# MLP norm factor: applied with the ReLU on the sums of the up products instead of on the inputs of the paired blocks

## The chip, the core and the metric

The kernel runs on one core of a Trainium2 chip. A core has five engines that run side by side, each with its own queue that is worked off in order: TensorE (PE, with its weight loads PEld), VectorE (DVE), ScalarE (ACT), GpSimd (POOL) and SyncE (SP), which here issues nearly all DMA transfers. They wait for each other through semaphores. The metric is the device time of one execution in microseconds (us); the kernel before takes 1254.85 us (median of three runs, 1254.52 to 1256.27).

## The reference

Two layers (DEPTH = 2) over 512 tokens of width 1024 in float32. Each layer mixes (attention, short convolution and RWKV heads, then an output projection) and then runs a squared-ReLU MLP behind an RMSNorm. The change touches the MLP alone:

```python
x = x + mixed @ w_out[l]
h = rms_norm(x, norm_mlp_g[l])
x = x + jnp.square(jax.nn.relu(h @ w_mlp_up[l])) @ w_mlp_down[l]
```

`rms_norm(x, g)` is x times a factor per token (one over the root of the mean square) times a weight g per feature. The factor is positive and is the same for all features of a token, so it can stand before or behind the product with `w_mlp_up`, and behind or inside the ReLU.

## The kernel before

Tokens lie on the free axis (512 columns), features on the 128 partitions: x is eight tiles of 128x512. TensorE multiplies in a reduced float32 form, so each operand is split into a high part (`hi`, a cast on ACT) and the rest (`lo`, a subtraction on DVE or POOL), and each product is three matmuls: hi x hi, lo x hi, hi x lo. Weights come in halves of 128x512: SP loads `raw`, ACT casts `whi`, DVE subtracts `wlo`, from rings of three buffers each (`weights`, L328 to L341). A half is used by 12 matmuls. A half's `whi` buffer can be written again only when TensorE has read it.

The mixing part of a layer has an order written out by hand (`ORDER`). It ends with the splits of x times g into `ahif`, `alof` (`inputs`, L721), the first three up products (`up_0` to `up_2`) and the norm's factor (`inner_norm`, L746): sums of squares on TensorE, a power on POOL, then `prbf`, a broadcast of the factor to all partitions in a PSUM bank, and its copy `rsf` in SBUF (L761).

The MLP part has no written order: the program's text is recorded and a scheduler lays the instructions on each engine's queue. It has three sections per layer.

- **The up section.** Eight groups of 128 up features are plain products of `ahif`, `alof` (`up`, L1394). PSUM banks come from a ring of four (`rp`, which `prbf` shares) for all but the first two. DVE multiplies the sum by `rsf` (L1402), ACT applies Relu (L1389), Square (L1391) and the cast `mh` (L1381), POOL makes `ml` (L1382). Meanwhile eight tiles `bn` are made on DVE: x times g times the factor, read from the PSUM bank `prbf` (L1415). From them come four sets of block differences `t` (L1421 to L1424) and their splits `thi`, `tlo` (L1428, L1429).
- **The first down products** (`down`, L1506). Each of eight groups takes 12 matmuls into one of two PSUM banks (`mm`), and DVE adds the sum to x (L1514). Beside them `parts_of` splits `bn` into `bhi`, `blo` (L1437, L1438), in the buffers that `ahif`, `alof` had.
- **The pairs** (`two`, L1440). The remaining 24 up groups are done two at a time with seven products of 256 columns in place of eight (a scheme of Strassen and Winograd): 12 matmuls each, from `bhi`, `blo` or `thi`, `tlo` and from weight sums that DVE makes. DVE adds the pieces to `c0` and `c1` (L1494, L1498, L1501), ACT applies Relu to them and to `pa`. After most pairs come four groups of `down`. There are 12 pairs per layer.

The last layer ends with `last_group` (the last down products, the final norm and the output).

Of the kernel before, what the change touches and what calls it, by code (L numbers as in the profile page):

```python
# [10 lines left out]
F32 = mybir.dt.float32  # L11
F32R = mybir.dt.float32r
# [3 lines left out]
AF = mybir.ActivationFunctionType  # L16
ALU = mybir.AluOpType
# [5 lines left out]
S = 512  # L23
P = 128
NK = D // P
NB = S // P
# [152 lines left out]
N_ONE = 8  # L179
# [7 lines left out]
C_GMIX, C_GMLP, C_SUB, C_CONV, C_MU = 0, 8, 16, 17, 23  # L187
# [81 lines left out]
def tile_trunk(ctx: ExitStack, tc: tile.TileContext, xT, wts, prm_d, cst_d, lora_d, gup_d, lam_d, fin_d, out):  # L269
    nc = tc.nc  # L270
    act, dve, pool = nc.scalar, nc.vector, nc.gpsimd
# [22 lines left out]
    cp = Pool(ctx.enter_context(tc.tile_pool(name="cp", bufs=1)), "cp")  # L294
# [10 lines left out]
    x = [cp.tile([P, S], F32, tag=f"x{j}", name=f"x{j}") for j in range(NK)]  # L305
# [58 lines left out]
    nrm = {}  # L364
# [198 lines left out]
    for l in range(L):  # L563
# [5 lines left out]
        with ExitStack() as mx:  # L569
# [176 lines left out]
            def inner_norm():  # L746
                key = f"f{l}"
                yield from got(nrm, "all" + key)
                pt = psum("rp", 4, f"pss{key}")
                for b in range(NB):  # L750
                    ins = pe.matmul(pt[:, b:b + 1], nrm[key][0][:, b * P:(b + 1) * P], ones1, start=True, stop=True)
                yield ins
                r = cp.tile([P, NB], F32, tag="rr", bufs=2, name=f"rr{key}")
                yield from root_steps(r, pt[:, :NB], NB)
                rb = psum("rp", 4, f"prb{key}")
                for b in range(NB):
                    ins = pe.matmul(rb[:, b * P:(b + 1) * P], r[:, b:b + 1].to_broadcast([P, P]), ident, start=True, stop=True)
                yield ins
                rs = cp.tile([P, S], F32, tag="rs", bufs=1, name=f"rs{key}")
                nrm["rs"] = rs, rb  # L760
                yield act.copy(rs, rb)  # L761

            def norm():
# [604 lines left out]
        with ExitStack() as mx:  # L1368
# [2 lines left out]
            H = S // 2  # L1371
            mids = []

            rs, rb = nrm["rs"]

            def kept(m):

# [7 lines left out]
            def square(cs, name):  # L1385

                r = fp.tile([P, S], F32, tag="r", bufs=2, name=f"r{name}")
                for i, c in enumerate(cs):
                    act.activation(r[:, i * H:i * H + c.shape[1]], c, AF.Relu)  # L1389
                m = fp.tile([P, S], F32, tag="m", bufs=3, name=f"m{name}")  # L1390
                act.activation(m, r, AF.Square)  # L1391
                kept(m)

            def up(i):  # L1394

                if i < NUP:
                    pt = ups[i]
                else:
                    pt = psum("rp", 4, f"up{l}_{i}")
                    mm3(pt, weights(wbase + NG_IN + NG_OUT + i), acts)  # L1400
                c = fp.tile([P, S], F32, tag="c0", bufs=2, name=f"c{l}_{i}")
                dve.tensor_tensor(c, pt, rs, ALU.mult)  # L1402
                square([c], f"{l}_{i}")

            bn, th = {}, {}

            def scaled_by_norm(j):
                if j == 0:  # L1410
                    fp.tile([P, 8], F32, tag="pad0", name=f"pad0_{l}")
                bn[j] = fp.tile([P, 2, H], F32, tag="shi" if j < 5 else "slo", bufs=5, name=f"bn{l}_{j}")
                if j == 5:
                    fp.tile([P, 24], F32, tag="pad1", name=f"pad1_{l}")
                dve.scalar_tensor_tensor(bn[j].rearrange("p a s -> p (a s)"), x[j], pr[:, C_GMLP + j:C_GMLP + j + 1], rb,  # L1415
                                         ALU.mult, ALU.mult)

            def blocks(k):
                b1, b2 = bn[k], bn[k + 4]
# [11 lines left out]
            bs = {}  # L1431

            def parts_of(j):

                n = 1 if j < 4 else 2
                hi, lo = bs[j] = [cp.tile([P, 2, H], F32R, tag=f"a{p}{j}", name=f"b{p}{l}_{j}") for p in ("hi", "lo")]
                act.copy(hi[:, :n], bn[j][:, :n])  # L1437
                dve.tensor_tensor(lo[:, :n], bn[j][:, :n], hi[:, :n].bitcast(F32), ALU.subtract)  # L1438

            def two(i0, i1):  # L1440

                n = f"{l}_{i0}"
                wg = wbase + NG_IN + NG_OUT

                def raw(i, a):
                    t = fp.tile([P, 4, P], F32, tag="sraw", bufs=6, name=f"raw{n}_{i}_{a}")
                    nc.sync.dma_start(t.rearrange("p k c -> p (k c)"), wts[wg + i, :, a * P:(a + 4) * P])
                    return t

                def both(src, name):  # L1450
                    hi, lo = [fp.tile([P, 4, P], F32R, tag=f"s{p}", bufs=5, name=f"s{p}{n}_{name}") for p in ("hi", "lo")]
                    act.copy(hi, src)  # L1452
                    dve.tensor_tensor(lo, src, hi.bitcast(F32), ALU.subtract)  # L1453
                    return hi, lo

                def sum_(name, a, b, op):
                    t = fp.tile([P, 4, P], F32, tag=name, name=f"{name}{n}")
                    dve.tensor_tensor(t, a, b, op)
                    return t

                def small(name):
                    return fp.tile([P, H], F32, tag=name, bufs=2, name=f"{name}{n}")

                def product(pt, w, moving, first=True):

                    whi, wlo = w
                    for k in range(4):
                        ahi, alo = moving(k)
                        pe.matmul(pt, whi[:, k], ahi, start=(first and k == 0), stop=False, skip_group_check=True)
                        pe.matmul(pt, whi[:, k], alo, start=False, stop=False, skip_group_check=True)  # L1470
                        pe.matmul(pt, wlo[:, k], ahi, start=False, stop=(k == 3), skip_group_check=True)

                blk = lambda d, q: lambda k: [p[:, q] for p in bs[4 * d + k]]
                smm = lambda q: lambda k: [p[:, q] for p in th[k]]
                pa, pb = [psum("rp", 4, f"p{i}{n}")[:, :H] for i in "ab"]
                pc = psum("at", 2, f"pc{n}")[:, :H]
                c0 = fp.tile([P, S], F32, tag="c0", bufs=2, name=f"c0{n}")
                w11 = raw(i0, 0)
                product(pa, both(w11, "p1"), blk(0, 0))
                p1 = small("p1")  # L1480
                act.copy(p1, pa)
                w21 = raw(i1, 0)
# [11 lines left out]
                dve.tensor_tensor(c0[:, :H], pc, p1, ALU.add)  # L1494
# [6 lines left out]
                dve.tensor_tensor(c0[:, H:], pb, u2, ALU.add)  # L1501
                square([c0], f"{n}_0")
                product(pa, both(w22, "p4"), smm(3), False)
                square([pa, c1], f"{n}_1")

            def down(h, js):  # L1506

                g, k0 = h // 2, 4 * (h % 2)
                for j in js:
                    pt = psum("mm", 2, f"dn{l}_{h}_{j}")  # L1510
                    mm3(pt, weights(wbase + NG_IN + NG_OUT + NG_UP + 8 * g + j, k0, k0 + 4), mids[4 * h:4 * h + 4], 4)
                    if h == 0:
                        parts_of(j)
                    dve.tensor_tensor(x[j], pt, x[j], ALU.add)  # L1514
# [12 lines left out]
            for p in range(N_TWO):  # L1527
# [76 lines left out]
```

## Time and profile before

| what | value |
|---|---|
| median of three runs | 1254.85 us (1254.52 to 1256.27) |
| the profiled execution | 1255.07 us, of which span 1253.1 us; 2.0 us lie around the span |
| granted TensorE clock | 0.997 of full speed |
| DMA | 127.92 MB, mean 102 GB/s |
| layer 0: up section, first down products, pairs | from about 291, 326.6 and 349.5 us |
| layer 1: the same | from about 907.5, 945.8 and 967.7 us |

A row of the engines' line gives busy time, its share of the span and the number of instructions. Rows of the timeline give start, duration, engine, line, operation, output<-inputs and, in brackets, how long the engine sat idle before it and what ended that. TensorE's matmuls overlap: one of 512 columns is shown as 0.39 us long, while the next starts 0.23 us later, so the distance from start to start is the measure of its pace.

### The profile page before, as it was taken

What the parts mean: (1) busy time and instruction counts of PE and PEld (TensorE: products, weight loads), DVE (VectorE), ACT (ScalarE), POOL (GpSimd) and SP (SyncE); (2) the same over time, 40 slices, a digit from 0 to 9 for tenths busy, and PEclk for the clock granted to TensorE, in tenths of its full rate; (3) what the DMA queues carried; (4) which work ended last, traced back from release to release, by engine and by line L of the source; (5) the groups of instructions that cost most, each with busy time, mean ns of one, the idle gap of its engine ahead of it and who ended that gap; (6) DMA issues with size and microseconds to landing.
All of it is one profiled execution on the core that took longest, in us unless ns stands there. A gap on an engine that the chain in (4) does not pass through costs nothing. (4 is left out here: it accounts for less than half of the span.)

```text
span 1253.1 us, 25011 instructions
## 1 busy us (share of the span) xinstructions
PE 1233.6 (98%) x9493; PEld 1055.0 (84%) x9493; DVE 903.3 (72%) x1731; ACT 697.5 (56%) x1476; POOL 358.2 (29%) x461
## 2 busy tenths in 40 slices
PE   9999999999999999999999999999999999999997
PEld 6888788788799999999778887888878999998987
DVE  6887888768967676764666777887598666666654
ACT  6785655546645454544475656464565545454553
POOL 1264637332301010101225455464221111111100
PEclk9999999999999999999999999999999999999998
DMA  6523323142332323221235233232423232323122
GB/s 214 162 91 93 113 87 107 53 143 84 128 100 94 110 93 110 93 93 35 78 109 161 80 119 108 91 88 71 141 84 135 93 109 94 108 95 108 53 76 76
DMA packets 84696, 127.92 MB, mean 102 GB/s; under 512 B 21472, under 2 KB 25568, under 8 KB 84576
## 3 DMA queue, kind: packets, MB, share of 16 engines
q1 hardware_dynamic: 83856, 125.77, 31.4%
q8 instruction: 75, 1.23, 0.4%
q10 hardware_dynamic: 720, 0.55, 0.1%
q14 instruction: 45, 0.37, 0.1%
HBM read 117.11 MB, written 9.18 MB: 101 GB/s over the span
## 5 line engine op out<-in xcount | busy, mean ns | idle before, releaser
L1382 POOL TENSOR_TENSOR ml<-m,mh 128x512 fp32r<-128x512 f32 x64 | 93.4, 1461 | 500.7 <-ACT mh L1381 482.7
L338 ACT CAST whi<-raw 128x512 fp32r<-128x512 f32 x142 | 88.0, 621 | 174.4 <-PE dn L282 159.0
L282 PE MATMUL dn<-mh,whi 128*128 128x512 f32 x448 | 175.1, 391 | 1.2 <-DVE x L1514 1.2
L282 PE MATMUL dn<-ml,whi 128*128 128x512 f32 x448 | 174.6, 390 | 0.0
L282 PE MATMUL dn<-mh,wlo 128*128 128x512 f32 x448 | 174.6, 390 | 0.0
L674 POOL TENSOR_TENSOR wlo<-raw,whi 128x512 fp32r<-128x512 f32 x84 | 110.5, 1316 | 189.2 <-ACT whi L662 159.4
L282 PE MATMUL pj<-ahim,whi 128*128 128x512 f32 x392 | 156.6, 399 | 1.0 <-DVE x L1514 0.9
L282 PE MATMUL pj<-ahim,wlo 128*128 128x512 f32 x392 | 156.7, 400 | 0.0
L282 PE MATMUL pj<-alom,whi 128*128 128x512 f32 x392 | 156.0, 398 | 0.0
L662 ACT CAST whi<-raw 128x512 fp32r<-128x512 f32 x142 | 87.5, 617 | 85.8 <-PE pj L282 29.8
L1514 DVE TENSOR_TENSOR x<-dn,x 128x512 f32<-128x512 f32 x112 | 76.7, 686 | 77.4 <-PE dn L282 77.4
L339 DVE TENSOR_TENSOR wlo<-raw,whi 128x512 fp32r<-128x512 f32 x142 | 113.4, 799 | 11.3 <-ACT whi L338 10.7
L1453 DVE TENSOR_TENSOR slo_p<-s,shi_p 128x512 fp32r<-128x512 f32 x96 | 70.9, 741 | 63.4 <-ACT shi_p L1452 60.8
L282 PEld LDWEIGHTS dn<-mh,whi 128*128 128x128 f32 x448 | 84.1, 188 | 19.9 <-issue 2.0
L282 PEld LDWEIGHTS dn<-mh,wlo 128*128 128x128 f32 x448 | 84.1, 188 | 17.9
L282 PEld LDWEIGHTS dn<-ml,whi 128*128 128x128 f32 x448 | 84.1, 188 | 16.5
L1452 ACT CAST shi_p<-s 128x512 fp32r<-128x512 f32 x96 | 59.1, 617 | 49.7 <-PE pa L282 38.1
L282 PEld LDWEIGHTS pj<-ahim,whi 128*128 128x128 f32 x392 | 73.8, 188 | 15.1 <-ACT whi L662 1.3
L282 PEld LDWEIGHTS pj<-alom,whi 128*128 128x128 f32 x392 | 73.9, 189 | 14.0 <-issue 0.5
L282 PEld LDWEIGHTS pj<-ahim,wlo 128*128 128x128 f32 x392 | 73.8, 188 | 14.0 <-DVE wlo L674 0.2
L282 PE MATMUL pa<-tlo,shi_p 128*128 128x256 f32 x288 | 81.4, 282 | 0.0
L282 PE MATMUL pa<-thi,shi_p 128*128 128x256 f32 x288 | 81.2, 282 | 0.0
(416 smaller groups left out, 3232.5 us busy)
## 6 DMA issues: line engine op xcount, KB each, us to landing
raw<-wts SPq DMA_DIRECT2D x389, 256.0 KB, 2.7
qs<-dqhi SPq DMA_DIRECT2D x24, 128.0 KB, 3.7
ks<-dkhi SPq DMA_DIRECT2D x24, 128.0 KB, 4.0
x<-xT SPq DMA_DIRECT2D x8, 256.0 KB, 4.6
dqhi<-qhi SPq DMA_DIRECT2D x6, 256.0 KB, 3.3
dqlo<-qlo SPq DMA_DIRECT2D x6, 256.0 KB, 3.4
dkhi<-khi SPq DMA_DIRECT2D x6, 256.0 KB, 2.7
dklo<-klo SPq DMA_DIRECT2D x6, 256.0 KB, 3.5
```

The lines of the kernel that those rows point to most:

```text
L282: ins = nc.tensor.matmul(*a, **k)
L338: act.copy(hi[:, :n], raw[:, :n])
L339: (pool if a and lean[0] else dve).tensor_tensor(lo[:, :n], raw[:, :n], hi[:, :n].bitcast(F32), ALU.subtract)
L662: yield act.copy(hi[:, k0:k1], raw[:, k0:k1])
L674: yield eng.tensor_tensor(lo[:, k0:k1], raw[:, k0:k1], hi[:, k0:k1].bitcast(F32), ALU.subtract)
L1382: pool.tensor_tensor(lo, m, hi.bitcast(F32), ALU.subtract)
L1452: act.copy(hi, src)
L1453: dve.tensor_tensor(lo, src, hi.bitcast(F32), ALU.subtract)
L1514: dve.tensor_tensor(x[j], pt, x[j], ALU.add)
```

## The change

The factor leaves the blocks' inputs and is applied to the sums, in the same instruction as the ReLU: `r = max(sum, 0) * rs`, on DVE, for the plain groups and for the pairs. So the pairs' blocks can be x times g without the factor: the products of plain blocks read `ahif`, `alof` (no second split, `parts_of` is gone), and `bn` is now made on ACT. Its bias operand `none`, a column of zeros computed from `rs`, makes it wait until the factor exists. The column takes one of the two buffers of the ring `rr`, which a table-loading Sqrt (L468, output `rrF`) uses too.

```diff
-                nrm["rs"] = rs, rb
+                nrm["rs"] = rs
...
-            rs, rb = nrm["rs"]
+            rs = nrm["rs"]
...
                 r = fp.tile([P, S], F32, tag="r", bufs=2, name=f"r{name}")
                 for i, c in enumerate(cs):
-                    act.activation(r[:, i * H:i * H + c.shape[1]], c, AF.Relu)
+                    q = slice(i * H, i * H + c.shape[1])
+                    dve.scalar_tensor_tensor(r[:, q], c, 0.0, rs[:, q], ALU.max, ALU.mult)
...
-                c = fp.tile([P, S], F32, tag="c0", bufs=2, name=f"c{l}_{i}")
-                dve.tensor_tensor(c, pt, rs, ALU.mult)
-                square([c], f"{l}_{i}")
+                square([pt], f"{l}_{i}")
...
+            none = cp.tile([P, NB], F32, tag="rr", bufs=2, name=f"none{l}")[:, :1]
+            dve.tensor_scalar(none, rs[:, :1], 0.0, None, ALU.is_lt)
-            def scaled_by_norm(j):
+            def by_gain(j):
...
-                dve.scalar_tensor_tensor(bn[j].rearrange("p a s -> p (a s)"), x[j], pr[:, C_GMLP + j:C_GMLP + j + 1], rb,
-                                         ALU.mult, ALU.mult)
+                act.activation(bn[j].rearrange("p a s -> p (a s)"), x[j], AF.Identity, scale=pr[:, C_GMLP + j:C_GMLP + j + 1],
+                               bias=none)
...
-            def parts_of(j):
-                n = 1 if j < 4 else 2
-                hi, lo = bs[j] = [cp.tile([P, 2, H], F32R, tag=f"a{p}{j}", name=f"b{p}{l}_{j}") for p in ("hi", "lo")]
-                act.copy(hi[:, :n], bn[j][:, :n])
-                dve.tensor_tensor(lo[:, :n], bn[j][:, :n], hi[:, :n].bitcast(F32), ALU.subtract)
...
-                blk = lambda d, q: lambda k: [p[:, q] for p in bs[4 * d + k]]
+                blk = lambda d, q: lambda k: [p[:, q * H:(q + 1) * H] for p in acts[4 * d + k]]
...
-                    if h == 0:
-                        parts_of(j)
...
-                for j in range(2 * max(i - 2, 0), min(2 * max(i - 1, 0), NK)):
-                    scaled_by_norm(j)
                 if i >= N_ONE - 4:
-                    blocks(i - N_ONE + 4)
+                    k = i - N_ONE + 4
+                    by_gain(k)
+                    by_gain(k + 4)
+                    blocks(k)
```

The scheduler lays the queues anew. Three places, as they stand before and after.

TensorE, layer 1, where `up_2` ends (a row's first name is the sum, behind the arrow the tokens' part and the weights' part). Before:

```order
L282 MATMUL up_2_11687<-alof_7_11628,whi_4_11671 128x512
L282 MATMUL up_2_11687<-ahif_7_11627,wlo_4_11673 128x512
L282 MATMUL up_4_11803<-ahif_0_11418,whi_0_11806 128x512
L282 MATMUL up_4_11803<-alof_0_11419,whi_0_11806 128x512
L282 MATMUL up_4_11803<-ahif_0_11418,wlo_0_11807 128x512
```

After:

```order
L282 MATMUL up_2_11641<-alof_7_11582,whi_4_11625 128x512
L282 MATMUL up_2_11641<-ahif_7_11581,wlo_4_11627 128x512
L282 MATMUL up_3_11697<-ahif_0_11372,whi_0_11700 128x512
L282 MATMUL up_3_11697<-alof_0_11373,whi_0_11700 128x512
L282 MATMUL up_3_11697<-ahif_0_11372,wlo_0_11701 128x512
```

Before, the first half of `up_4` stood ahead of all of `up_3`; now it stands behind it. All other matmuls of the kernel keep their order (those of the pairs with `ahif`, `alof` in the place of `bhi`, `blo`).

DVE, layer 0, where the first down group is added to x (`x_69` is the first tile of x). Before:

```order
L339 TENSOR_TENSOR wlo_0_4534<-raw_0_4531,whi_0_4533 128x512
L1438 TENSOR_TENSOR blo_6_4646<-bn_6_4348,bhi_6_4645 128x512
L1438 TENSOR_TENSOR blo_7_4670<-bn_7_4350,bhi_7_4669 128x512
L1514 TENSOR_TENSOR x_69<-dn_0_0_4482,x_69 128x512
L1453 TENSOR_TENSOR slo_8_p_4681<-raw_8_8_0_4678,shi_8_p_4680 128x512
L339 TENSOR_TENSOR wlo_0_4558<-raw_0_4555,whi_0_4557 128x512
L1453 TENSOR_TENSOR slo_8_p_4705<-s_8_4702,shi_8_p_4704 128x512
L1453 TENSOR_TENSOR slo_8_p_4725<-s_8_4722,shi_8_p_4724 128x512
L1514 TENSOR_TENSOR x_70<-dn_0_1_4506,x_70 128x512
```

After:

```order
L1390 SCALAR_TENSOR_TENSOR r_7_4444<-up_7_4407,rsf_4109 128x512
L339 TENSOR_TENSOR wlo_0_4512<-raw_0_4509,whi_0_4511 128x512
L1505 TENSOR_TENSOR x_69<-dn_0_0_4468,x_69 128x512
L339 TENSOR_TENSOR wlo_0_4532<-raw_0_4529,whi_0_4531 128x512
L1505 TENSOR_TENSOR x_70<-dn_0_1_4488,x_70 128x512
```

The eight `blo` are gone, and the splits of the first pair's weights (`slo_8`) have moved up into the up section; between two sums added to x stands one `wlo`.

DVE, layer 0, the end of the third pair (number 10) and the start of the down groups behind it. Before:

```order
L1501 TENSOR_TENSOR c_10_5155<-pb_10_5153,u_10_5218 128x256
L1458 TENSOR_TENSOR s_12_5678<-s_12_5658,raw_12_12_0_5634 128x512
L1453 TENSOR_TENSOR slo_11_p_5462<-raw_11_11_4_5459,shi_11_p_5461 128x512
L1453 TENSOR_TENSOR slo_11_p_5481<-s_11_5478,shi_11_p_5480 128x512
L1514 TENSOR_TENSOR x_69<-dn_2_0_5311,x_69 128x512
L339 TENSOR_TENSOR wlo_0_5375<-raw_0_5372,whi_0_5374 128x512
```

After:

```order
L1494 TENSOR_TENSOR c_10_5109<-pb_10_5107,u_10_5172 128x256
L1451 TENSOR_TENSOR s_12_5632<-s_12_5612,raw_12_12_0_5588 128x512
L1390 SCALAR_TENSOR_TENSOR r_10_0_5232<-c_10_5109,rsf_4109 128x512
L1390 SCALAR_TENSOR_TENSOR r_10_1_5256<-pa_10_5106,rsf_4109 128x256
L1390 SCALAR_TENSOR_TENSOR r_10_1_5256<-c_10_5211,rsf_4109 128x256
L1446 TENSOR_TENSOR slo_11_p_5416<-raw_11_11_4_5413,shi_11_p_5415 128x512
L1446 TENSOR_TENSOR slo_11_p_5435<-s_11_5432,shi_11_p_5434 128x512
L1451 TENSOR_TENSOR s_12_5671<-raw_12_12_0_5588,raw_12_24_0_5608 128x512
L1505 TENSOR_TENSOR x_69<-dn_2_0_5265,x_69 128x512
```

Three instructions `r` stand in the queue ahead of the next pair's splits; the second of them waits for the pair's last product in `pa`.

More of the change, by code (lines that the diff above doesn't have):

```diff
@@ L1400, in up @@
                     mm3(pt, weights(wbase + NG_IN + NG_OUT + i), acts)
-                c = fp.tile([P, S], F32, tag="c0", bufs=2, name=f"c{l}_{i}")
-                dve.tensor_tensor(c, pt, rs, ALU.mult)
-                square([c], f"{l}_{i}")
+                square([pt], f"{l}_{i}")
             bn, th = {}, {}
-            def scaled_by_norm(j):
+            none = cp.tile([P, NB], F32, tag="rr", bufs=2, name=f"none{l}")[:, :1]
+            dve.tensor_scalar(none, rs[:, :1], 0.0, None, ALU.is_lt)
+            def by_gain(j):
                 if j == 0:
                     fp.tile([P, 8], F32, tag="pad0", name=f"pad0_{l}")
-                bn[j] = fp.tile([P, 2, H], F32, tag="shi" if j < 5 else "slo", bufs=5, name=f"bn{l}_{j}")
-                if j == 5:
+                bn[j] = fp.tile([P, 2, H], F32, tag="shi" if j < 4 else "slo", bufs=5, name=f"bn{l}_{j}")
+                if j == 4:
                     fp.tile([P, 24], F32, tag="pad1", name=f"pad1_{l}")
-                dve.scalar_tensor_tensor(bn[j].rearrange("p a s -> p (a s)"), x[j], pr[:, C_GMLP + j:C_GMLP + j + 1], rb,
-                                         ALU.mult, ALU.mult)
+                act.activation(bn[j].rearrange("p a s -> p (a s)"), x[j], AF.Identity, scale=pr[:, C_GMLP + j:C_GMLP + j + 1],
+                               bias=none)
             def blocks(k):
@@ L1429, in blocks @@
                     dve.tensor_tensor(lo[:, u], t[i], hi[:, u].bitcast(F32), ALU.subtract)
-            bs = {}
-            def parts_of(j):
-                n = 1 if j < 4 else 2
-                hi, lo = bs[j] = [cp.tile([P, 2, H], F32R, tag=f"a{p}{j}", name=f"b{p}{l}_{j}") for p in ("hi", "lo")]
-                act.copy(hi[:, :n], bn[j][:, :n])
-                dve.tensor_tensor(lo[:, :n], bn[j][:, :n], hi[:, :n].bitcast(F32), ALU.subtract)
             def two(i0, i1):
```

## Prediction

> **What bounds the kernel now.** I read the page's totals, then its chain of waits, then what TensorE itself waited for, and last the timeline at those places.
>
> ```profile
> span 1253.1 us, 25011 instructions
> PE 1233.6 (98%) x9493; PEld 1055.0 (84%) x9493; DVE 903.3 (72%) x1731; ACT 697.5 (56%) x1476; POOL 358.2 (29%) x461
> ...
> PE 37%; DVE 1%; ACT 0%; issue 0%; POOL 0%; POOLq 0%; DVEq 0%
> ...
> 945.83 21.83 PE dn L282 x96
> ...
> 977.66 10.93 PE dn L282 x48
> ```
>
> The chain lies on TensorE almost alone, and in the pairs and the down groups it has no holes: 48 matmuls take 10.93 us, 0.228 us each. The change leaves their number as it is, so a saving on DVE or ACT is worth only what it closes of TensorE's holes, and a cost there is free until it opens one. The waits of TensorE in the MLP are few:
>
> ```profile
> PE dn L282 <- DVE x L1514: 1.2, 3, 0.7
> PE up L282 <- DVE wlo L339: 0.9, 1, 0.9
> PE up L282 <- ACT whi L338: 0.5, 1, 0.5
> PE up L282 <- DVE bn L1415: 0.4, 1, 0.4
> ```
>
> Their places, from TensorE's timeline, the `up` rows in layer 1, the `dn` rows in layer 0:
>
> ```profile
> 915.61 0.39 PE L282 MATMUL up<-ahif,wlo 128*128 128x512 f32 x1
> 916.53 0.50 PE L282 MATMUL up<-ahif,whi 128*128 128x512 f32 x1 [0.53 <-ACT whi L338]
> 916.86 0.40 PE L282 MATMUL up<-alof,whi 128*128 128x512 f32 x1
> 918.14 0.50 PE L282 MATMUL up<-ahif,wlo 128*128 128x512 f32 x1 [0.88 <-DVE wlo L339]
> ...
> 920.32 0.39 PE L282 MATMUL up<-ahif,wlo 128*128 128x512 f32 x1
> 921.09 0.47 PE L282 MATMUL up<-ahif,whi 128*128 128x512 f32 x1 [0.38 <-DVE bn L1415]
> ...
> 331.77 0.39 PE L282 MATMUL dn<-mh,wlo 128*128 128x512 f32 x1
> 332.82 0.47 PE L282 MATMUL dn<-mh,whi 128*128 128x512 f32 x1 [0.66 <-DVE x L1514]
> ...
> 335.42 0.39 PE L282 MATMUL dn<-mh,wlo 128*128 128x512 f32 x1
> 335.83 0.47 PE L282 MATMUL dn<-mh,whi 128*128 128x512 f32 x1
> ```
>
> Each hole is the distance of two starts less 0.23. Around 916 us: 0.92, 0.33 and 1.28 make 0.69 + 0.10 + 1.05 = 1.84 us. At 921: 0.77, so 0.54. In layer 0: 1.05 and 0.41, so 0.82 + 0.18 = 1.00. Together 3.38 us. Behind them stands a full DVE in the up section, and an idle one in the pairs (its busy time in a stretch of each):
>
> ```profile
> 293.00:326.00 33.00, 32.53 (x56) 1.00 0.30 99
> ...
> 967.66:988.59 20.93, 14.27 (x23) 1.00 0.31 100
> ```
>
> **The change part by part: what closes.** The 1.84 us are a matter of order. `up_4`'s first half follows `up_2` at once, and its `whi` needs the buffer that `up_2`'s last half has just given back:
>
> ```profile
> 915.86 0.62 ACT L338 CAST whi<-raw 128x512 fp32r<-128x512 f32 x1 [1.58 <-issue]
> ```
>
> ACT casts it 0.25 us after TensorE's last start there, DVE's `wlo` comes later still. Now `up_3` stands there; its first half gets the buffer of `up_2`'s first half, 12 matmuls (2.7 us) earlier, and `up_4` starts 24 matmuls later. I count all 1.84 us as gained. The 0.54 us are the PSUM bank of `prbf`, held until the last `bn` has read it. After the change its only reader is the copy `rsf`, so it is free some 12 us before: 0.54 gained. The 1.00 us in layer 0 are DVE's backlog:
>
> ```profile
> 330.80 1.28 DVE L1438 TENSOR_TENSOR blo<-bn,bhi 128x512 fp32r<-128x512 f32 x2
> 332.00 0.68 DVE L1514 TENSOR_TENSOR x<-dn,x 128x512 f32<-128x512 f32 x1
> ```
>
> The first down sum waits behind `blo`, and TensorE's third group for its bank. The `blo` go, and so do the eight `bn` from DVE's queue:
>
> ```profile
> L1415 DVE SCALAR_TENSOR_TENSOR bn<-x,prm,prbf 128x512 f32<-128x512 f32 x16 | 11.2, 738 | 0.0
> ...
> L1438 DVE TENSOR_TENSOR blo<-bn,bhi 128x512 fp32r<-128x512 f32 x8 | 5.1, 679 | 0.0
> ```
>
> Per layer that is 8 x 0.74 = 5.9 and, with four `blo` of 512 columns and four of 256 (taken at half), 2.7 + 1.4 = 4.1 us less; the eight `r` that replace the `c` cost 0 to 0.06 us more each (0.68 of L1438's row to 0.74 of L1415's). About 9.5 us less on DVE, ahead of the sum that was late by some 2 us: 1.00 gained.
>
> **What is added.** Bounds from the nearest rows:
>
> ```profile
> L1389 ACT ACTIVATE r<-c 128x512 f32<-128x512 f32 x40 | 25.3, 633 | 19.0 <-DVE c L1402 9.5 <-DVE c L1501 8.9
> ...
> L730 ACT ACTIVATE ahif<-x,prm 128x512 fp32r<-128x512 f32 x16 | 11.0, 714 | 1.8 <-PE po L282 1.2 <-DVE x L715 0.6
> ...
> L915 ACT ACTIVATE t<-av,drv,prm 128x512 f32<-128x512 f32 x6 | 4.8, 803 | 0.0
> ...
> L1494 DVE TENSOR_TENSOR c<-pc,p 128x256 f32<-128x256 f32 x24 | 10.2, 424 | 5.9 <-PE pc L282 5.9
> ...
> L468 ACT ACT_TABLE_LOAD x1 | 1.3, 1283 | 0.0
> ```
>
> *`bn` on ACT* lies between L730 (one column operand, 0.71) and L915 (two, 0.80); it has two, so 0.80, eight times 6.4 us per layer, against eight Relu less (5.0): +1.4 us, and the eight `bhi` go behind it. The column `none` (four bytes a partition on DVE) is 0.1 to 0.2 us and delays the first `bn` alone. *The Sqrt table* is loaded before at the start of layer 1 and, after other tables, once more at the end, where ACT is waiting anyway; now it is loaded once, behind `rsf` in layer 1: 1.28 us plus 0.2 for `rrF` on ACT, at a delicate place. I place it by hand:
>
> ```profile
> 907.82 0.59 ACT L761 COPY rsf<-prbf 128x512 f32<-128x512 f32 x1 [0.88 <-PE prbf L282]
> ```
>
> `rsf` ends at 908.4, the table and `rrF` at 909.9, then a Square, `bn`, `mh`, Square, `whi` (second half of `up_3`), `mh`, and `whi` of its first half: at 0.63 us each (0.80 for `bn`) 914.5. TensorE gets there at 915.61 + 0.23 = 915.84. So 1.3 us are in hand, 0.4 to 0.5 more for the `wlo` behind it, which TensorE needs two matmuls later and DVE makes at 0.68 us. Between 0 and the whole 1.5 us may come through; I take 0.
>
> *The pairs.* DVE gets one `r` of 512 and two of 256 columns per pair: 0.74 + 0.42 + 0.42 = 1.6 us (1.5 by the `TENSOR_TENSOR` rows), ACT loses its Relus. DVE has 20.93 - 14.27 = 6.7 us idle in such a period, so its total fits. What counts is the queue, since the second `r` waits for the pair's last product and the splits and x sums stand behind it:
>
> ```profile
> 421.64 0.68 DVE L1458 TENSOR_TENSOR s<-s,raw 128x512 f32<-128x512 f32 x1
> ...
> 425.07 0.90 DVE L1453 TENSOR_TENSOR slo_p<-s,shi_p 128x512 fp32r<-128x512 f32 x1 [2.15 <-ACT shi_p L1452]
> 425.89 0.68 DVE L1514 TENSOR_TENSOR x<-dn,x 128x512 f32<-128x512 f32 x1
> ...
> 428.21 0.69 DVE L1514 TENSOR_TENSOR x<-dn,x 128x512 f32<-128x512 f32 x1
> ```
>
> The 1.6 us fall into the 2.15 us in which DVE waits for a cast that ACT makes late, behind Relus and Squares; without the Relus that cast comes before the Squares. Without this cover the x sum would end at 426.6 + 1.6 = 428.2, about when the third down group needs its bank (the second's sum can start at 428.21), so even then little shows. I take 0; were all 1.6 us to come through in 24 pairs, it would be 38 us. POOL's and SP's queues have the same work; a few loads for the second pair are issued earlier.
>
> **Sum.** 1255.07 - 1.84 - 0.54 - 1.00 = 1251.7 us for an execution like the profiled one (span 1249.7). The median of the runs is 0.2 below it, so **1251.5 us**.
>
> **The rivals.**
>
> *The holes only move (20%).* For it: three weight buffers per ring leave TensorE two halves ahead, whatever the order; ACT and DVE now hand `bn`, `t`, `thi`, `tlo` to each other with the `whi` and `wlo` queued between them. Against it: 9.5 us less on DVE. If the 1.84 us stay as another wait, the run gives 1251.5 + 1.8 = 1253.3; if all stay, the change does nothing for the time: 1254.85.
>
> *ACT becomes late in the up section (12%, slower).* Place: `whi` behind `bn`, which waits for the factor. Price: if in each of the four block steps one `bn` and one `t` to `thi` handover (0.8 + 0.7 us) stay ahead of the `whi` that TensorE needs, that is 6 us per layer, less the 1.3 us in hand and the two halves of lead (2.7 us): 2 us per layer beyond the old holes, 4 in all: 1254.85 + 4 = 1259. It decides from 1.3 us on. Against it: behind the place in question ACT (the fourth pair of numbers) is far from full:
>
> ```profile
> 921.00:946.00 25.00, 24.91 (x110) 20.67 (x111) 22.85 (x39) 17.83 (x34) 6.02 (x5) 1.00 0.29 95
> ```
>
>
> *DVE's queue in the pairs opens a hole in each (5%, slower).* Place: the x sum behind `r`, price: what it is late beyond 1.6 us, in 22 periods with down groups. For it, POOL and DVE stretch each other:
>
> ```profile
> L1453 DVE TENSOR_TENSOR slo_p<-s,shi_p x96: 675/693/1348, 333.8 to 1191.4; 128x512 fp32r<-128x512 f32 x96
> ```
>
> If `r` stretched so, 0.65 us more, then 22 x 0.65 - 3.4 = 11 us: 1266. Against it: in the trace POOL's `ml` of a pair comes only after that pair's `r`. The Trainium skill ("SBUF — State Buffer", "Who interferes with whom") says that a VectorE instruction with two SBUF inputs and a GpSimd instruction that reads SBUF exclude each other for the whole instruction; that speaks against the change, since two of the three `r` have two SBUF inputs where ACT's Relu had one. The largest value in the row, 1348 ns beside a median of 693, agrees with it; by that rule the 11 us would follow only if `r` met `ml`.
>
> **How the numbers follow.** The forecast has 63%: 1250 to 1252.6 by itself (an unseen small start more or less). The range reaches over the moved holes up to 1256 and down to 1249.8; most of the two slower cases stays outside. A measurement here tells about 0.2%, 2.5 us, from no change: faster is below 1252.3, nearly all of the forecast and a little of the second case (61%); same is the rest of both (22%); slower 17%.
>
> **What would show it.** TensorE's waits: the four rows above gone, the first pair of layer 1 about 2.4 us earlier after `prbf` than now, that of layer 0 1.0 us. DVE in a pair period near 15.9 us of 20.93, with `r` inside the wait before the x sum. Wrong would be: a wait of `up` for `whi` or `wlo` of another group, a `dn` that waits for x behind a pair, or a pair period longer than 20.93 us.

## The result, and the profile after

The changed kernel takes 1252.11 us (median of 22 runs), the kernel before 1254.01 us in the same comparison; the ratio is 0.9981 with a 95% interval of 0.9974 to 0.9989, so 1.4 to 3.3 us are gained. A second comparison, with the experiments below, has 1250.62 against 1254.37 us, 0.9973 (0.9963 to 0.9983). The forecast was 1251.5 us.

The page of the changed kernel, its totals (engine, busy us, share of the span, instructions):

```profile
span 1252.3 us, 24947 instructions
PE 1234.0 (99%) x9493; PEld 1057.9 (84%) x9493; DVE 915.4 (73%) x1773; ACT 665.7 (53%) x1386; POOL 374.2 (30%) x461
```

TensorE does the same work; DVE has 42 instructions more and ACT 90 fewer. The two profiled spans alone (1253.1 and 1252.3 us) would hide most of the result, because single executions of one kernel lie 5 to 6 us apart in the first comparison. So the profiles are read stretch by stretch, between starts of TensorE's instructions that both kernels have. What TensorE waited for in the changed kernel's MLPs (us in total, times, longest), all rows on `up`, `dn` and `pa`:

```profile
PE up L282 <- DVE wlo L339: 0.6, 1, 0.6
...
PE dn L282 <- DVE x L1505: 0.5, 2, 0.3
PE pa L282 <- DVE c L1491: 0.4, 1, 0.4
```

The waits for `whi` and `bn` are gone, and of the `dn` rows only two small ones are left, at the very end of layer 0, where before has them too (0.17 and 0.32 us). The `wlo` and the `pa` row are new ones. TensorE's timeline at the old places, layer 1 at 916 us and layer 0 at 331 us, shows the closed holes as an even pace:

```profile
916.81 0.39 PE L282 MATMUL up<-ahif,whi 128*128 128x512 f32 x1
917.04 0.39 PE L282 MATMUL up<-alof,whi 128*128 128x512 f32 x1
917.27 0.39 PE L282 MATMUL up<-ahif,wlo 128*128 128x512 f32 x1
...
331.31 0.39 PE L282 MATMUL dn<-mh,wlo 128*128 128x512 f32 x1
331.54 0.39 PE L282 MATMUL dn<-mh,whi 128*128 128x512 f32 x1
```

And the two new holes, at the end of layer 1's up section and in layer 0's first pair:

```profile
941.52 0.39 PE L282 MATMUL up<-alof,whi 128*128 128x512 f32 x1
942.46 0.51 PE L282 MATMUL up<-ahif,wlo 128*128 128x512 f32 x1 [0.55 <-DVE wlo L339]
942.80 0.40 PE L282 MATMUL up<-ahif,whi 128*128 128x512 f32 x1
...
356.32 0.28 PE L282 MATMUL pb<-ahif,slo_p 128*128 128x256 f32 x1
356.97 0.39 PE L282 MATMUL pa<-thi,shi_p 128*128 128x256 f32 x1 [0.37 <-DVE c L1491]
```

Here is the reason of the first one. DVE's timeline, and below it POOL's, in the 2.5 us ahead of it:

```profile
939.43 0.68 DVE L1446 TENSOR_TENSOR slo_p<-raw,shi_p 128x512 fp32r<-128x512 f32 x1
940.03 1.77 DVE L1446 TENSOR_TENSOR slo_p<-s,shi_p 128x512 fp32r<-128x512 f32 x1
941.73 0.68 DVE L339 TENSOR_TENSOR wlo<-raw,whi 128x512 fp32r<-128x512 f32 x1
```

```profile
939.41 1.84 POOL L1382 TENSOR_TENSOR ml<-m,mh 128x512 fp32r<-128x512 f32 x1 [1.66 <-ACT mh L1381]
```

The two `slo_p` have one shape. The first starts with POOL's `ml` and takes 0.68 us, while that `ml` takes 1.84 us where the shortest takes 1.29. The second takes 1.77 us and ends 0.55 us after `ml` does. So DVE and POOL seem to take turns here. The `wlo` that TensorE needs stands behind the second: 1.1 us too late. The second hole is a load that lands late: DVE's sum for the third pair waits for it, and this pair's `c` stands behind that sum.

The stretches, in us, are the basis of all that follows: "up" from the first `prbf` matmul to the first down matmul, "down" from there to the first pair, "pair 1" from there to the second pair; "MLPs" is both layers from `prbf` to their ends (layer 0: the next layer's first mixing product; layer 1: the last sums of the norm). E5 and E4 are second profiles of the kernel before and of the change.

| kernel | layer 0: up | down | pair 1 | layer 1: up | down | MLPs | ratio to before (95%) |
|---|---|---|---|---|---|---|---|
| before | 36.51 | 23.19 | 20.92 | 39.04 | 21.83 | 670.6 | |
| E5, before again | 36.51 | 23.20 | 20.93 | 39.06 | 21.76 | 670.7 | 0.9994 (0.9984 to 1.0003) |
| the change | 36.64 | 21.77 | 21.57 | 37.29 | 21.77 | 668.5 | 0.9981 (0.9974 to 0.9989) |
| E4, the change again | 36.61 | 21.77 | 21.65 | 37.25 | 21.77 | 668.5 | 0.9973 (0.9963 to 0.9983) |
| E1, bank free early | 37.18 | 23.09 | 20.92 | 37.26 | 23.94 | 672.3 | 1.0010 (1.0000 to 1.0021) |
| E2, plain groups only | 36.51 | 22.91 | 20.93 | 39.82 | 22.03 | 672.3 | 1.0022 (1.0011 to 1.0033) |
| E3, pairs and blocks only | 36.59 | 22.46 | 21.63 | 36.46 | 23.62 | 670.2 | 1.0002 (0.9991 to 1.0013) |
| E6, `bn` on DVE | 37.93 | 22.18 | 20.92 | 37.74 | 22.52 | 670.4 | 0.9994 (0.9983 to 1.0004) |
| E7, `none` by itself | 37.51 | 21.78 | 21.65 | 37.38 | 21.77 | 669.2 | 1.0023 (1.0012 to 1.0033) |
| E8, `ml` on DVE | 36.51 | 21.77 | 20.93 | 36.41 | 21.77 | 666.5 | 0.9961 (0.9949 to 0.9973) |
| E9, pairs' `r` twice | 36.61 | 21.76 | 21.62 | 37.26 | 21.76 | 669.4 | 0.9984 (0.9973 to 0.9996) |
| E10, plain `r` twice | 36.51 | 23.41 | 20.93 | 36.79 | 24.15 | 671.0 | 1.0001 (0.9991 to 1.0011) |
| E11, `none` in an old buffer | 36.64 | 21.76 | 21.67 | 36.79 | 21.77 | 667.9 | 0.9970 (0.9960 to 0.9980) |
| E12, before with `ml` on DVE | 36.51 | 21.77 | 20.93 | 39.45 | 21.77 | 670.5 | 0.9993 (0.9983 to 1.0003) |

Two profiles of one kernel agree within 0.1 us in the MLPs, and the MLPs' sum goes roughly with the measured ratio. The exception is E7, which loses elsewhere. One of the eleven executions of E7 took 4279 us and is not in its ratio. The change gains 2.2 us there, 0.6 in layer 0 and 1.6 in layer 1.

### The profile page after: what moved, and what is told of

It is laid out like the page before. It is cut to its first block, busy times and chain, and to the rows that moved or that the text cites. A ratio compares the mean times of both kernels' runs of the same rounds, so it can differ in the third digit from the quotient of the medians.

```text
span 1252.3 us, 24947 instructions
## 1 busy us (share of the span) xinstructions
PE 1234.0 (99%) x9493; PEld 1057.9 (84%) x9493; DVE 915.4 (73%) x1773; ACT 665.7 (53%) x1386; POOL 374.2 (30%) x461
## 5 line engine op out<-in xcount | busy, mean ns | idle before, releaser
L1382 POOL TENSOR_TENSOR ml<-m,mh 128x512 fp32r<-128x512 f32 x64 | 110.3, 1739 | 481.2 <-ACT mh L1381 375.4
L1446 DVE TENSOR_TENSOR slo_p<-s,shi_p 128x512 fp32r<-128x512 f32 x96 | 67.9, 708 | 18.1 <-ACT shi_p L1445 15.5
```

The lines of the kernel that those rows point to most:

```text
L1382: pool.tensor_tensor(lo, m, hi.bitcast(F32), ALU.subtract)
```

## The experiments

### E1 to E4: the parts of the change

One caution holds for all that follows. For every altered program the scheduler lays the queues of DVE, ACT and SP anew, so an experiment changes a load and the order of these queues together. TensorE's order stays one of two: before's in E2 and E12, the change's in all others, E1 included (E5 and E4 repeat their kernels).

Theory at this point: a part of the sum belongs to the bank of `prbf` and can be had alone. In E1, `bn` reads the copy `rsf` in SBUF; nothing else in the program's text differs from before:

```diff
-                nrm["rs"] = rs, rb
+                nrm["rs"] = rs
...
-            rs, rb = nrm["rs"]
+            rs = nrm["rs"]
...
-                dve.scalar_tensor_tensor(bn[j]..., x[j], pr[:, C_GMLP + j:C_GMLP + j + 1], rb,
+                dve.scalar_tensor_tensor(bn[j]..., x[j], pr[:, C_GMLP + j:C_GMLP + j + 1], rs,
```

> Before, with one thing changed: bn reads the SBUF copy rsf instead of the PSUM bank of prbf. Theory (the bank): with the copy as the bank's only reader, up_3's first half stands ahead of up_4's again, and both layer-1 holes go: from prbf to the first matmul of the first pair it is 58.5 us (before 60.87, less 1.84 and 0.54); layer 0 keeps its two dn holes (1.00 us); the time is 2.4 us below before, ratio 0.9981. Rival (the holes come from DVE's and ACT's load, which this leaves as it is): the stretch stays above 60 us, with up waiting for whi or wlo of another group, ratio 0.9995 to 1.0.

Layer 1's up stretch is 37.26 us, as short as the change's: the order is back to `up_3` ahead of `up_4`, and both holes are gone. So who reads the bank is what had turned the order. But nothing is gained. TensorE's timeline in layer 1's first down groups:

```profile
950.65 0.39 PE L282 MATMUL dn<-mh,wlo 128*128 128x512 f32 x1
952.47 0.47 PE L282 MATMUL dn<-mh,whi 128*128 128x512 f32 x1 [1.43 <-DVE x L1514]
```

TensorE arrives 1.8 us earlier and finds DVE as late as ever, with the last five `blo` (2.9 us) still queued ahead of the first x sum: the down stretch grows from 21.8 to 23.94 us. The theory names the cause of the two holes and is wrong on their price.

E2 is before with the plain groups' `r` on DVE, all else as it was; E3 is the reverse, the change with the plain groups as before. This is E2's main cut (`squared` is the part of `square` behind the ReLU):

```diff
-                c = fp.tile([P, S], F32, tag="c0", bufs=2, name=f"c{l}_{i}")
-                dve.tensor_tensor(c, pt, rs, ALU.mult)
-                square([c], f"{l}_{i}")
+                r = fp.tile([P, S], F32, tag="r", bufs=2, name=f"r{l}_{i}")
+                dve.scalar_tensor_tensor(r, pt, 0.0, rs, ALU.max, ALU.mult)
+                squared(r, f"{l}_{i}")
```

> Before, with only the plain up groups changed: DVE's r (ReLU times factor) in place of DVE's c and ACT's Relu; bn, parts and pairs as before. Theory (the bank): bn still reads the bank, up_4's first half still stands ahead of up_3, DVE's queue is as full as before: the stretch prbf to first pair of layer 1 60.3 to 60.9 us, layer 0 keeps its dn holes, ratio 0.9995 to 1.0005. Rival (the holes come from ACT's casts behind its Relus): whi is earlier by up to a Relu (0.63 us), the stretch below 60.2 us, ratio 0.9990 or less.

> The change without its first part: pairs and blocks as in the change (bn without the factor, on ACT; r with the factor on DVE in the pairs; bhi and blo gone), plain up groups as before (c on DVE, Relu on ACT). Theory: nearly all of the change's gain is here: layer 0's dn holes gone (1.0 to 1.3 us), layer 1's 1.84 and 0.54 gone; ratio 0.9975 to 0.9985. If the wlo hole at the end of layer 1's up section (0.83 us in the change's profile) comes from POOL's ml beside DVE's full queue, it stays within 0.4 us of that; if it comes from r with its two inputs in the plain groups, it is gone. Rival (the gain needs the plain groups' r): ratio 0.9990 or more.

E2 loses: its holes at 916 to 921 us are the same ones, two of them larger (`wlo` 1.20 us, `bn` 0.84 us), and the `whi` wait is unchanged at 0.5 us, so ACT's Relus were not what held the casts. E3 gains nothing that the runs can tell. It has the shortest up stretch of layer 1 but for one (36.46 us) and no `wlo` hole there, and then loses 1.9 us in the down groups:

```profile
947.07 0.39 PE L282 MATMUL dn<-ml,whi 128*128 128x512 f32 x1
948.14 0.50 PE L282 MATMUL dn<-mh,wlo 128*128 128x512 f32 x1 [0.68 <-DVE wlo L339]
```

DVE's rows ahead of this hole are of the kind seen in the change. A weight sum `s` takes 1.54 us where others take 0.68, it ends 0.56 us after an `ml` of POOL (945.49 to 946.93), and the awaited `wlo` stands behind it:

```profile
945.95 1.54 DVE L1459 TENSOR_TENSOR s<-raw,raw 128x512 f32<-128x512 f32 x1 [0.17 <-DMA raw<-wts]
947.41 0.68 DVE L339 TENSOR_TENSOR wlo<-raw,whi 128x512 fp32r<-128x512 f32 x1
```

So alone the first half of the change loses 1.6 us in the MLPs and the second gains 0.5; together they gain 2.2. Of the four theories only E3's rival, that the gain needs the plain groups' `r`, fits its ratio; both of E2's missed. Why the plain groups' `r` is a loss with the old blocks and a gain with the new ones was not taken further apart.

> The changed kernel once more, unaltered, for a second profile. Theory: the wlo hole at the end of layer 1's up section is the order's and stays (0.6 to 1.0 us in starts); the stretch at the granted clock of 0.5 to 0.75 after the sums of layer 1's mixing norm, the late load at 686 us and the late loads in the first pairs are this one execution's and are gone or elsewhere: from layer 0's last down group to prbf of layer 1 as before (289.1 us within 0.5) instead of 2.2 us longer. Rival (they belong to the change): all of them at the same places. Ratio 0.9975 to 0.9988.

The changed kernel again, unaltered: the `wlo` hole is there (0.55 us idle), and so is the late load in layer 0's first pair (0.47); they belong to the change. The slow stretch and the late load in layer 1's mixing are gone (280.76 us from layer 0's end to `prbf`, where the first profile took 284.12 and before 281.91): these were that execution's.

### E5, E6, E10, E12: DVE's load

New theory: the holes are DVE's backlog; where they open is the order's doing, how large they are in sum is DVE's whole time from `prbf` to the first pair. E5 is the kernel before once more:

> The kernel before once more, unaltered, as a null test and for a second profile. From prbf to the first mixing product of the next layer 334.7 us in layer 0, from prbf to the last sums of the norm 335.95 us in layer 1, both within 0.4 us; the mixing of layer 1 281 to 284 us, with or without a stretch at half the granted clock after its sums; ratio 0.9990 to 1.0010. Rival (the profile of before was an exception): the holes at 916 to 921 us of layer 1 differ by more than 0.5 us in sum.

It repeats the first profile within 0.1 us in every stretch. E6 takes the change and puts `bn` back on DVE, E10 makes each plain `r` twice, E12 takes the kernel before and makes the plain groups' `ml` on DVE:

```diff
-                act.activation(bn[j]..., x[j], AF.Identity, scale=pr[:, C_GMLP + j:C_GMLP + j + 1], bias=none)
+                dve.tensor_scalar(bn[j]..., x[j], pr[:, C_GMLP + j:C_GMLP + j + 1], none, ALU.mult, ALU.add)
```

> The change with its eight bn per layer put back on DVE (one input times the column), ACT freed of them; bhi and blo stay gone. Theory (DVE's whole load of the up section and first down group sets the holes): 3.3 to 5.9 us more on DVE per layer bring back 1 to 2.5 us of holes over the two layers, in the up section or in the first down sums; ratio 0.9980 to 1.0000. Rival (the order of the weights halves alone): no more holes than the change has, ratio 0.9970 to 0.9980.

```diff
-                    dve.scalar_tensor_tensor(r[:, q], c, 0.0, rs[:, q], ALU.max, ALU.mult)
+                    for _ in range(2 if name in plain else 1):
+                        dve.scalar_tensor_tensor(r[:, q], c, 0.0, rs[:, q], ALU.max, ALU.mult)
```

> The change with each r of the plain up groups made twice on DVE (eight times 0.68 = 5.4 us more per layer, same values). Theory (DVE's whole load of the up section sets the holes): 1 to 2 us more per layer, layers' MLP together 670.5 to 672.5 us where the change has 668.5; ratio 0.9990 to 1.0015. Rival (what the change gained is the order of the weights' halves and the bank alone): MLP together within 0.6 us of the change's, ratio 0.9965 to 0.9985.

```diff
-                pool.tensor_tensor(lo, m, hi.bitcast(F32), ALU.subtract)
+                (dve if i < N_ONE else pool).tensor_tensor(lo, m, hi.bitcast(F32), ALU.subtract)
```

> The kernel before with the ml of the plain up groups on DVE instead of POOL, nothing else. Theory (POOL's ml costs DVE as much as making ml itself): DVE is no later than before, layer 0's first down group 22.0 to 23.2 us (23.2 before); layer 1 keeps its order and bank holes, 38.0 to 39.2 us from prbf to the first down group; ratio 0.9985 to 1.0000. Rival (this alone gives what the change gives): 36.5 to 37.3 us there, ratio 0.9980 or less.

Read together, from one row each (`plain` in E10's cut holds the names of the plain groups): busy times in layer 1 from `prbf` to the first pair (the stretch, its length, then PE, PEld, DVE, ACT, POOL with their instructions, the granted clock, DMA share and GB/s). Before (E5):

```profile
905.22:966.04 60.82, 59.02 (x260) 48.05 (x261) 52.62 (x87) 37.01 (x68) 14.41 (x9) 1.00 0.35 109
```

The change (E4):

```profile
903.94:962.96 59.02, 58.47 (x260) 48.22 (x261) 45.62 (x72) 35.53 (x62) 16.28 (x9) 1.00 0.37 112
```

E3:

```profile
907.66:967.74 60.08, 59.03 (x261) 48.06 (x262) 45.74 (x72) 39.53 (x70) 14.57 (x9) 1.00 0.35 111
```

E6:

```profile
904.49:964.75 60.26, 59.14 (x261) 48.03 (x261) 50.38 (x80) 30.65 (x54) 15.44 (x9) 1.00 0.34 110
```

E10:

```profile
904.87:965.81 60.94, 59.19 (x260) 48.00 (x261) 50.05 (x80) 35.07 (x62) 17.29 (x9) 1.00 0.36 108
```

The third pair of numbers, DVE, goes with the length in four of these rows, though not in proportion: 45.6 us and 59.0; 50.1 to 50.4 and 60.3 to 60.9; 52.6 and 60.8. Eight more instructions of 0.68 us on DVE (E10) cost 1.9 us here and 2.5 us in both MLPs, the whole gain. Eight `bn` of 0.6 us more on DVE (E6) cost 1.9 us in both MLPs, although ACT then has 5 us less to do. TensorE's order is the change's in both, so that order alone does not give the gain. E3 is off the line: DVE as in the change, ACT 4 us more, and 1.1 us longer, with the stretched `s` shown above. E12 closes layer 0's 1.42 us, makes layer 1's old holes 0.4 us larger and has a late load in one pair (0.6 us): its ratio is in the theory's range, its two stretches just outside of it on either side, and it does not give what the change gives. It also refutes the second half of the theory: from `prbf` to the first pair of layer 0, DVE is busy for 53.17 us in E12 and 53.13 us in before, yet E12 has no hole there (58.28 us against 59.70). Its first x sum starts 3.1 us after the first down matmul, before's 5.4 us. So DVE's whole time does not set the size of the holes. What counts is how late one awaited instruction is, by what stands ahead of it and by what is stretched there.

### E8: the remaining hole

The 1.77 us row above says that POOL's `ml` and DVE hold each other up. If so, making `ml` on DVE costs DVE nothing. E8 is the change with the line of E12:

> The change with the ml of the plain up groups on DVE instead of POOL (eight per layer); the pairs' ml stay on POOL. Theory (POOL's ml and DVE hold each other up: one DVE instruction beside an ml takes 1.2 to 1.8 us instead of 0.68): those long DVE rows go, DVE's busy time in the up section of layer 1 stays within 2 us although it has 5.4 us more to do, and the wlo hole (0.83 us in starts) shrinks to below 0.3; ratio 0.9965 to 0.9980. Rival (DVE's queue is full, whatever POOL does): 5.4 us more on DVE open 1 to 3 us of holes per layer, ratio 0.9990 to 1.0020.

```profile
905.31:963.49 58.18, 58.18 (x261) 48.31 (x262) 44.62 (x80) 35.65 (x62) 1.28 (x1) 1.00 0.35 114
```

DVE does 80 instructions in 44.62 us, where the change does 72 in 45.62: eight more, 5.4 us of work, in 1.0 us less. None of these 80 takes over 0.7 us by itself. Each `ml` on POOL had cost DVE 0.8 us. TensorE is busy for the whole stretch, and all four up and down stretches of both layers and the first pairs are without holes. This version is faster than the kernel before: 1250.28 us against 1254.93, ratio 0.9961 (0.9949 to 0.9973). Against the change it has 2.0 us less in the MLPs; it was not run against it directly, and its interval overlaps that of the change's second comparison.

### E7 and E11: the table load

The change had moved a load of ACT's tables behind `rsf` in layer 1. E7 gives `none` a buffer of its own, E11 a dead old one:

```diff
-            none = cp.tile([P, NB], F32, tag="rr", bufs=2, name=f"none{l}")[:, :1]
+            none = cp.tile([P, NB], F32, tag="none", bufs=1, name=f"none{l}")[:, :1]
```

```diff
-            none = cp.tile([P, NB], F32, tag="rr", bufs=2, name=f"none{l}")[:, :1]
+            none = cp.tile([P, L, 2], F32, tag="lexp", name=f"none{l}")[:, 0, :1]
```

> The change with the column none in a buffer of its own instead of the ring of rr, so that the loads of ACT's tables go back to where they stand in before (early in layer 1 and at the end) and none comes behind rsf in layer 1. Theory (the load behind rsf is covered, as I took it): prbf to first down group of layer 1 within 0.3 us of the change's 37.3, ratio 0.9970 to 0.9985. Rival (the load behind rsf makes ACT and then DVE late, and the wlo hole at the end of the up section is its echo): that stretch 36.5 to 36.8 us, 0.5 to 0.8 us gained, but up to 1.3 us lost at the end, where the table is then loaded.

> The change with the column none in an old dead buffer (that of lexp), so that no tile moves and no table load stands behind rsf in layer 1. Theory (the buffer of its own cost by moving what lies behind it, 2.6% on every product that reads ahi and alo): the first mixing takes 289 us again and not 292, the products of the up section are back at 0.228 us; and if the table load was the cause of the wlo hole, prbf to first down group of layer 1 is 36.4 to 36.7 us instead of the change's 37.3; ratio 0.9960 to 0.9980. Rival (the slower products come with the other places of the table loads): 292 us and 0.234 us a product again, ratio 1.001 to 1.003.

Both move the table loads back to where they are in before. E11 has layer 1's up stretch at 36.79 us, 0.5 below the change's, and no `wlo` hole; both layers' MLPs take 0.6 us less. That prices the load together with the new order of the queues: some DVE and ACT instructions of layer 1's up section stand elsewhere too. E8 keeps the load behind `rsf` and has no hole either, while E11 keeps `ml` on POOL, so the hole was not seen without both. E7 has no holes there either, and yet 37.38 us, with layer 0's up stretch and both mixings longer too; by the ratios it is 6 to 7 us slower than E11, which neither theory of E7 had. The instructions of the two stand in the same order on every engine; what differs is told in the last section.

### E9: the cover in the pairs

```diff
-                    dve.scalar_tensor_tensor(r[:, q], c, 0.0, rs[:, q], ALU.max, ALU.mult)
+                    for _ in range(1 if name in plain else 2):
+                        dve.scalar_tensor_tensor(r[:, q], c, 0.0, rs[:, q], ALU.max, ALU.mult)
```

> The change with each r of the pairs made twice on DVE (1.55 us more per pair, same values). Theory (the pairs have cover): DVE's busy time in a pair period rises from 15.4 to about 17.0 us of 20.93, the period stays 20.93 and the stretches from the second pair to the end of each layer stay at 254.05 and 254.15 to 254.45 us; ratio 0.9965 to 0.9985. Rival (DVE's queue in the pairs is at its edge): the x sum behind the second r comes late, a dn hole of 0.3 to 1.0 us in each of 22 periods, 7 to 22 us, ratio above 1.003.

One pair period of the changed kernel, and one of E9:

```profile
966.83:987.76 20.93, 20.93 (x135) 19.02 (x134) 15.43 (x26) 9.45 (x18) 3.47 (x2) 1.00 0.35 103
```

```profile
969.50:990.43 20.93, 20.93 (x134) 19.01 (x133) 17.58 (x29) 9.79 (x18) 3.11 (x2) 1.00 0.33 100
```

DVE's 2.1 us more leave the period as it was. What follows the first pair is 0.2 us longer in layer 0 and 0.8 us in layer 1; the one large hole there, 0.46 us in one pair, is a `c` behind a late load again. No period has a hole behind an x sum.

## Why the prediction was right, and where it was not

**The time.** The forecast's gain of 3.4 us, ratio 0.9973, is the second comparison's value and just outside the first's interval. The MLPs' 2.2 us lie within both. The sum was made of closed holes only; more closed than it said, and a part came back. That the forecast meets the second comparison so closely is therefore luck: where the sum applies, 2.2 us were gained and not 3.4. The direction and the four closed waits were foretold. Of its signs of being wrong, two came: `up` waits for a `wlo` of another group, and two pair periods are longer than 20.93 us (21.57 in layer 0, 21.22 in layer 1). The first pair comes 1.8 us earlier after `prbf` in layer 1 (2.4 foretold) and 1.3 us in layer 0 (1.0).

**Layer 1, 1.84 and 0.54 us.** From `prbf` to the matmul after the last of these holes it was 14.46 us (906.63 to 921.09) and is 11.92 (907.61 to 919.53): 2.54 closed where 2.38 were counted. The step "The 1.84 us are a matter of order" is right for where the hole stood, and it is one cause with the 0.54: the bank's reader turns the order (E1). The step "I count all 1.84 us as gained" is the one that needed DVE's relief, which the sum used only for layer 0. In E1, without that relief, 2.2 us are closed by the same matmul, and the down stretch behind it is 2.1 us longer.

**Layer 0, 1.00 us.** Measured 1.42 in the down stretch: the term was 0.4 us too small, since it had the two large holes of the backlog and not the steps of just under 0.1 us at the matmuls behind them, 0.3 us in sum. The mechanism, `bn` and `blo` off DVE, has E6 and E10 for it: with 4.4 to 4.8 us put back on DVE, most or all of the gain is gone. It is not the only way: E12 closes the same hole with `bn` and `blo` still on DVE. The relief was taken too large. About 9.5 us per layer were foretold; from `prbf` to the first pair DVE's busy time falls from 52.6 to 45.6 us in layer 1 and from 53.1 to 45.8 in layer 0, 7.0 and 7.3 us.

**What was added.** `bn` on ACT was taken at 0.80 us and measured, with `r` beside it:

```profile
L1417 ACT ACTIVATE bn<-x,none,prm 128x512 f32<-128x512 f32 x16 | 12.7, 809 | 0.2 <-DVE none L1408 0.2
...
L1390 DVE SCALAR_TENSOR_TENSOR r<-up,rsf 128x512 f32<-128x512 f32 x16 | 10.9, 681 | 1.3 <-PE up L282 1.3
```

The table load came where it was placed by hand, behind `rsf`:

```profile
908.80 0.59 ACT L761 COPY rsf<-prbf 128x512 f32<-128x512 f32 x1 [0.86 <-PE prbf L282]
909.40 1.28 ACT L468 ACT_TABLE_LOAD   x1
910.70 0.20 ACT L468 ACTIVATE rrF<-ones 128x1 f32<-128x1 f32 x1
```

It did not delay the `whi` at 916 us, as worked out. But by E11 it and the order that comes with it cost 0.5 us some 30 us later, in the hole at 942 us, together with POOL's `ml`. By that price "I take 0" of a range of 0 to 1.5 was 0.5 too little.

**The pairs, 0 us.** Right: the period is 20.93 us with DVE at 15.43 (15.9 foretold), and twice the `r` still fits (E9). Only the first pair of layer 0 has a hole, 0.65 us in starts, and that is a late load. It is there in both profiles of the change and in E3, E7, E9 and E11 (21.57 to 21.67 us), not in E6, E8 and E10, nor with the old blocks; what makes the load late was not settled.

**The rivals.** "The holes only move" was partly true: about 1.8 of the 4.0 us that closed are back, as the `wlo` hole (0.83 us in starts), the late load (0.65) and smaller ones. That is where the forecast and the MLPs' 2.2 us part. ACT was not late: no wait of TensorE in the MLPs names it, and the new hole is DVE's. The rule of the Trainium skill ("SBUF — State Buffer", "Who interferes with whom") on VectorE with two SBUF inputs and GpSimd was weighed at the wrong place. In the pairs it costs nothing. In the up section, which the forecast read as a matter of DVE's sum alone, it is what is left: the trace agrees with the rule (1.77 us for an `slo_p` that ends right behind an `ml`, 0.68 for the one before it), and E8 prices it, 0.8 us of DVE for each `ml`.

## What to carry to other kernels

A hole's releaser tells where a backlog shows, not what it is worth: before counting a hole as gained, ask how much earlier the next awaited instruction would have to be, and what stands ahead of it in its engine's queue. The engine's whole busy time is a hint and no measure: E12 and before have the same on DVE in layer 0, and only one has a hole. The halves of a change need not add up: here one alone lost, the other gained little, and together they gained more than their sum; why was not settled. Work that was put on POOL to spare DVE can cost DVE more than doing it, where both read SBUF at the same time (E8).

## What the hardware showed that was not expected

**Where a tile begins.** E7 and E11 have the same tables and the same instructions on TensorE; in E7 the small buffer moves what lies behind it in the pool, the weights `whi` and `wlo` and also `mh` and `ml`, by 32 bytes a partition, while `ahi` and `alo` stay. In 20 us of layer 0's up section (columns as in the rows of E5 above), E7 first, then E11:

```profile
295.00:315.00 20.00, 20.00 (x87) 16.10 (x86) 19.16 (x35) 17.70 (x31) 7.68 (x4) 1.00 0.26 82
```

```profile
295.00:315.00 20.00, 20.00 (x90) 16.57 (x89) 19.97 (x35) 16.64 (x29) 8.37 (x5) 1.00 0.26 81
```

TensorE is never idle in either, at full granted clock, and starts 87 matmuls where E11 starts 90; by the starts in the whole up section, holes left out, 0.2332 us each and 0.2270. The mixing products are slower too (the first mixing takes 292.05 us, E11's 289.30). The down products, 0.227 us in both, are not, nor are the pairs' products of 256 columns that read `ahif`, `alof` and the moved weights (0.118 us in both). Only this one shift was tried, so the rule behind it is open.

**After a hole of 1.6 us the clock was halved in half of the cases.** At the start of layer 1's mixing TensorE waits for a sum, 1.6 us in ten of the fourteen profiles and 0.5 us in four. After the long wait the granted clock fell to 0.5 for 3.4 us in five of the ten (the change's first profile, E1, E2, E3, E8), never after the short one. The first profile of the change, then E4, each the 3.40 us from 2.2 us after the wait:

```profile
631.50:634.90 3.40, 3.40 (x13) 2.96 (x13) 0.00 (x0) 0.65 (x2) 1.94 (x4) 0.53 0.25 95
```

```profile
631.19:634.59 3.40, 3.40 (x21) 2.94 (x20) 0.69 (x1) 1.52 (x3) 2.31 (x5) 1.00 0.14 50
```

In the first, 13 matmul instructions against 21 in the same time, at a clock of 0.53. From the end of the wait to the product behind the last `pw` the change's first profile takes 17.81 us (629.31 to 647.12) and E4, the same kernel, 16.20 (628.99 to 645.19). These 1.6 us are most of the change's own effect, and they lie between two executions of one kernel. The Trainium skill ("TensorE: Matmul & The Clock Gate", "Part 1: The HAM clock gate") has the clock halved after at least one idle window of about 3.4 us; here a wait of 1.6 us was followed by it in half of the cases.

**One `ml` took 3.5 times as long as the shortest.** POOL's `ml` takes 1.29 us at the least. In the up section of the changed kernel, among DVE's instructions, one is shown with 4.51 us (below). In sum POOL loses less than DVE, as far as its rough spans tell: by the rows of E4 and E8 its eight `ml` of layer 1 take 15.0 us, 4.7 more than eight times 1.29, while DVE loses 6.4.

```profile
933.24 4.51 POOL L1382 TENSOR_TENSOR ml<-m,mh 128x512 fp32r<-128x512 f32 x1 [4.15 <-ACT mh L1381]
```
